# A gated DeltaNet layer: convolution taps in PSUM, triangular solve on blocks of 16, and an earlier place for the solve

## The chip, the cores and the metric

The kernel runs on one core of one Trainium2 chip. The metric is the device time of one execution in microseconds (us). Before the change three runs took 1976.09, 1970.93 and 1973.98 us, median 1973.98.

## The reference

A two-layer backbone on 640 tokens (128 of a context, 512 of a sample), width 1024. Layer 0 mixes with a state-space model and attention, layer 1 with a bidirectional gated DeltaNet; an MLP follows each. The change lies in the DeltaNet:

```python
qkv = jax.nn.silu(_dwconv(proj[..., :3 * D_MODEL], conv_w))      # 5 taps along the tokens
q, k, v = split(qkv); q, k = l2norm(q) * DK ** -0.5, l2norm(k)
a_mat = jnp.where(tri_strict, (kb @ k.T) * decay, 0.0)           # per chunk, kb = k * beta
t_mat = triangular_solve(eye + a_mat, eye)                       # (I + A)^-1
u_c, w_c = t_mat @ (v * beta), t_mat @ (kb * exp(gcum))
# per chunk, in order:
v_new = u_i - w_i @ s
o = (q_i * exp(g_i)) @ s + attn_i @ v_new
s = s * exp(g_last) + (k_i * exp(g_last - g_i)).T @ v_new
out = (rmsnorm(o) * silu(z)) @ w_out
```

There are 8 heads of 128 and two directions, forward and backward.

## The kernel before

All tokens are columns: an activation is a set of tiles of 128 features by 640 tokens. A projection (`gemm`, `mm_step`, L205 to L207) splits weights and activations in a high and a low fp32r part and makes three matmuls of 320 columns per pair of 128x128 weight block and half; a tile of 128 outputs takes 48 of them. `weight` (L193 to L196) loads a block, ScalarE rounds the high part (L194), POOL forms the low one (L196).

The layer's method `odd` lets 33 tiles of the in-projection run: tile 0 holds the gates, 1 to 24 are four pairs of heads with six tiles each (`gdn_project`: k, k, q, q, v, v, m = 0 to 5), 25 to 32 are the gate z (`zproj`). For each pair, in words of the code:

- `gdn_project.ev` takes a tile from its PSUM bank ("pg") to `cb`, runs the five taps of the convolution there (L1319 ScalarE, L1322 VectorE, on 642 columns), for some tiles one tap through ScalarE and POOL (L1325, L1326), then tanh (L1328) and the closing multiply, on POOL for m 2 and 3 (L1332, L1333), else on VectorE (L1335, L1336). Then come square sums (L1272), normalising (L1278, L1285, L1290) and transposes to token order (L1299).
- `gdn_group` makes, for each chunk of 128 tokens, four matrices (two heads, two directions): Gram products (L1395), decay (L1400, L1401) and transposes (L1407). The strictly triangular 32x32 diagonal blocks go to `ub`, 80 of them on 80 partitions.
- `gdn_blocks` inverts these blocks by 31 steps of one multiply (L1425) and one subtract (L1427) on VectorE and stores them (`dd`, L1431).
- `gdn_inverse` loads them (`gcm`, L1439), spreads them over block-diagonal tiles by a mask on POOL (L1453) and transposes on VectorE (L1454), and merges 32 to 64 to 128 by small matmuls (helper at L1458) with ScalarE copies between.
- `gdn_chain` runs the chunks: `prep` (L1562 to L1579; the decay of the queries is multiplied on POOL at L1567), and per link L1615, L1620 (VectorE), L1625, L1627 (ScalarE), L1631 and L1632, L1643, L1646 (VectorE). A link needs the state that the link before it leaves.

Behind the z tiles the `gated` products (L1680 to L1689) are projected by `wouto`, four head tiles first and the rest in `odd_out`. Fillers (`mod_half`, L269, L282) load and compute the modulation of the MLP, 14 of them near the end of the layer.

No order is written out by hand. A tile scheduler sets each engine's order from data dependence and from priorities: groups are raised by 1000, the solve of blocks by 3000, inverse and chain by 10000, z tiles lowered by 3000 below that. The rings of the pools then decide when a tile is free: PSUM has the tags "pg", "pa", "pb" and "pc" with two banks each, SBUF has one ring per name with its `bufs`.

```python
for j in range(31):
    n, m = 31 - j, j + 1
    t = tmp[:, :n * m].rearrange("p (a b) -> p a b", b=m)
    V.tensor_tensor(t, ub[:, j, j + 1:32]..., D[:, j, 0:m]..., op=ALU.mult)
    V.tensor_tensor(D[:, j + 1:32, 0:m], D[:, j + 1:32, 0:m], t, op=ALU.subtract)
```

Of the kernel before, what the change touches and what calls it, by code (L numbers as in the profile page):

```python
# [11 lines left out]
F32 = mybir.dt.float32  # L12
# [8 lines left out]
T = 640  # L21
HB = 320
# [126 lines left out]
class Build:  # L149
# [1098 lines left out]
    def gdn_project(self, pr, hn, P, first=None, mid=None):  # L1248
# [45 lines left out]
        def tok(ty):  # L1294
            for part in range(3):
# [7 lines left out]
                if part < 2:  # L1303
                    nc.scalar.activation(dst[part][:, 1:5], pv, AF.Copy)
                else:
                    for hh in range(2):
                        V.tensor_copy(dst[hh][:, 0], pv[:, hh])
        def ev(m, h, p):
# [9 lines left out]
            cv = self.tl([128, 642], "cv")  # L1318
            nc.scalar.activation(cv, cb[m][:, 0:642], AF.Identity, scale=cw[:, 0:1])  # L1319
            split = m > 3 and pr > 0  # L1320
            for t in range(1, 4 if split else 5):
                V.scalar_tensor_tensor(cv, cb[m][:, t:t + 642], cw[:, t:t + 1], cv, op0=M, op1=AD)  # L1322
            if split:
                cy = cb[m][:, 4:646]
                nc.scalar.activation(cy, cy, AF.Identity, scale=cw[:, 4:5])  # L1325
                nc.gpsimd.tensor_tensor(cv, cv, cy, op=AD)  # L1326
            th = cb[m][:, 0:642]
            nc.scalar.activation(th, cv, AF.Tanh)  # L1328

            if m in (2, 3):  # L1330
                nc.scalar.activation(th, th, AF.Identity, bias=1.0)
                nc.gpsimd.tensor_tensor(cv[:, 0:128], th[:, 0:128], cv[:, 0:128], op=M)  # L1332
                nc.gpsimd.tensor_tensor(cv[:, 128:T], th[:, 130:642], cv[:, 130:642], op=M)  # L1333
            else:
                V.scalar_tensor_tensor(cv[:, 0:128], th[:, 0:128], 1.0, cv[:, 0:128], op0=AD, op1=M)  # L1335
                V.scalar_tensor_tensor(cv[:, 128:T], th[:, 130:642], 1.0, cv[:, 130:642], op0=AD, op1=M)  # L1336
# [78 lines left out]
    def gdn_blocks(self, pr, ub, P):  # L1415
# [18 lines left out]
    def gdn_inverse(self, pr, ud, dd, P):  # L1434
# [3 lines left out]
        cm = P.tile([128, 20, 32], F32, name="gcm")  # L1438
        nc.sync.dma_start(out=cm, in_=self.ap(dd, 0, [[32, 128], [4096, 20], [1, 32]]))  # L1439
# [5 lines left out]
        mask = self.cst[:, 404:532].rearrange("p (b j) -> p b j", b=4).unsqueeze(1).to_broadcast([128, 2, 4, 32])  # L1445

        D = P.tile([128, 5, 4, 128], F32, name="gD")
        TT = P.tile([128, 5, 4, 128], F32, name="gTT", bufs=2)
        two = lambda t, c, d: t[:, c, 2 * d:2 * d + 2].rearrange("p u j -> p (u j)")
        for c in range(5):  # L1450
            for d, a, b in ((0, D, TT), (1, TT, D)):
                src = cm[:, 4 * c + 2 * d:4 * c + 2 * d + 2].unsqueeze(2).to_broadcast([128, 2, 4, 32])
                G.tensor_tensor(a[:, c, 2 * d:2 * d + 2].rearrange("p u (b j) -> p u b j", b=4), src, mask, op=ALU.mult)  # L1453
                V.transpose(two(b, c, d), two(a, c, d))  # L1454
        CH = [(c, hh) for c in range(5) for hh in range(2)]

        def mm(out, l, r, col):
            nc.tensor.matmul(out, l, r, start=True, stop=True, tile_position=(0, col))  # L1458

        def bank(n):  # L1460
            return self.ps("pb")[:, :320].rearrange("p (c h j) -> p c h j", c=5, h=2)


        p = bank(0)
        for c, hh in CH:
            for a in (0, 64):
                x, y = slice(a, a + 32), slice(a + 32, a + 64)
                mm(p[y, c, hh], uo[:, 0, c, hh, a:a + 32], D[:, c, hh, x], a + 32)
# [53 lines left out]
    def gdn_chain(self, pr, pd, TT, P, roles, bank):  # L1522
# [23 lines left out]
        def prep(t):  # L1546
# [9 lines left out]
            if t:  # L1556
# [9 lines left out]
                for u in range(4):  # L1566
                    nc.gpsimd.tensor_tensor(gq[:, u], gq[:, u], lds[u][2 + u % 2], op=M)  # L1567
# [432 lines left out]
```

## Time and profile before

| | us |
|---|---|
| median of three runs | 1973.98 |
| the profiled execution | 1975.42 |
| its span, first to last instruction | 1973.2 |
| TensorE busy in the span | 1798.4 |
| the DeltaNet layer, first tile to the next statistics | 882.3 to 1502.5 |
| in it: TensorE busy | 533.3 |
| in it: VectorE busy | 456.8 |
| in it: ScalarE and POOL busy | 288.4, 284.8 |

One execution was profiled. Engines are PE (TensorE), DVE (VectorE), ACT (ScalarE), POOL and SP; PE's weight loads (PEld) run beside its matmuls. Busy time of matmuls counts overlapping records, so a busy PE may still be short of work; the start of one record to the start of the next shows its pace. An fp32 matmul leaves two records. A wait for several semaphores is put down to the last one.

### The profile page before, as it was taken

Reading aid. Unit: us, or ns where it says so; the run is one execution under the profiler, and the core shown is the slowest. Engines: PE = TensorE matmul, PEld = TensorE weight load, DVE = VectorE, ACT = ScalarE, POOL = GpSimd, SP = SyncE. Lnnn points to the kernel's source line nnn. Section 1 sums busy time; section 2 is a strip of 40 time slices with the busy share of each in tenths; the row PEclk is TensorE's granted clock in tenths of the full one; section 3 lists DMA queues with packets and bytes.
Section 4 is the critical chain, followed back from the end, with each engine's and each line's share of the span. In section 5 each row is a group of like instructions: output and inputs, shape, how many; then the busy total and the mean of one; then the engine's idle time right before and its main releaser. Section 6 shows DMA issues by size and latency. Waiting matters only on the chain. (4 is left out here: it accounts for less than half of the span.)

```text
span 1973.2 us, 35750 instructions
## 1 busy us (share of the span) xinstructions
PE 1798.4 (91%) x13556; PEld 1696.1 (86%) x13556; DVE 1279.3 (65%) x2797; ACT 875.5 (44%) x1956; POOL 760.1 (39%) x609
## 2 busy tenths in 40 slices
PE   5789799989999999997878888798989899999998
PEld 3789677978999999997877888787878799999997
DVE  8998777269273644547589988674667927364553
ACT  4344466344243443535454455344324425344362
POOL 2522101541343343453455555522245334343451
PEclk9989899999999999998998999999999999999999
DMA  8446886533332222332576468758844122222221
GB/s 319 131 122 167 248 264 205 201 121 126 109 117 76 77 85 82 135 117 72 163 208 197 117 196 239 222 166 269 274 137 149 54 97 76 86 76 86 76 97 54
DMA packets 206983, 286.60 MB, mean 145 GB/s; under 512 B 54878, under 2 KB 138236, under 8 KB 206812
## 3 DMA queue, kind: packets, MB, share of 16 engines
q1 hardware_dynamic: 206812, 284.33, 45.4%
q8 instruction: 107, 1.75, 0.4%
q14 instruction: 64, 0.52, 0.1%
HBM read 228.87 MB, written 46.82 MB: 140 GB/s over the span
## 5 line engine op out<-in xcount | busy, mean ns | idle before, releaser
L196 POOL TENSOR_TENSOR wlo<-raw,whi 128x1024 fp32r<-128x1024 f32 (+1 forms) x153 | 359.3, 2351 | 509.1 <-ACT whi L194 462.3
L194 ACT ACTIVATE whi<-raw 128x1024 fp32r<-128x1024 f32 (+1 forms) x153 | 153.1, 1001 | 329.1 <-PE pg L206 146.8
L207 PE MATMUL pg<-hidh,wlo 128*128 128x320 f32 (+2 forms) x576 | 178.8, 311 | 0.6 <-POOL wlo L196 0.6
L205 PE MATMUL pg<-hidh,whi 128*128 128x320 f32 (+2 forms) x576 | 179.0, 311 | 0.0
L206 PE MATMUL pg<-hidl,whi 128*128 128x320 f32 (+2 forms) x576 | 178.9, 311 | 0.0
L423 DVE SCALAR_TENSOR_TENSOR x<-pg,mod,x 128x128 f32<-128x128 f32 (+2 forms) x132 | 53.7, 436 | 182.2 <-PE pg L207 182.2
L205 PE MATMUL pg<-h10h,whi 128*128 128x320 f32 x472 | 158.4, 336 | 14.7 <-DVE cb L1722 7.0
L207 PE MATMUL pg<-h10h,wlo 128*128 128x320 f32 x472 | 155.4, 329 | 1.7 <-POOL wlo L196 1.7
L206 PE MATMUL pg<-h10l,whi 128*128 128x320 f32 x472 | 155.7, 330 | 0.0
L205 PE MATMUL pa<-hidh,whi 128*128 128x320 f32 x448 | 138.0, 310 | 1.1 <-ACT whi L194 1.1
L207 PE MATMUL pa<-hidh,wlo 128*128 128x320 f32 x448 | 138.4, 309 | 0.0
L206 PE MATMUL pa<-hidl,whi 128*128 128x320 f32 x448 | 138.2, 309 | 0.0
L423 DVE SCALAR_TENSOR_TENSOR x<-pa,mod,x 128x128 f32<-128x128 f32 (+2 forms) x108 | 43.9, 435 | 133.1 <-PE pa L207 133.1
L508 POOL TENSOR_TENSOR wq<-S,wq 128x512 fp32r<-128x512 f32 x52 | 71.3, 1371 | 115.3 <-ACT wq L507 115.3
L205 PEld LDWEIGHTS pg<-h10h,whi 128*128 128x128 f32 x472 | 95.8, 203 | 18.3 <-DVE cb L1722 8.0
L207 PEld LDWEIGHTS pg<-hidh,wlo 128*128 128x128 f32 x576 | 108.2, 188 | 1.6 <-POOL wlo L196 1.1
L205 PEld LDWEIGHTS pg<-hidh,whi 128*128 128x128 f32 x576 | 108.3, 188 | 0.9 <-issue 0.8
L206 PEld LDWEIGHTS pg<-hidl,whi 128*128 128x128 f32 x576 | 108.2, 188 | 0.4 <-DVE hidl L569 0.3
L1322 DVE SCALAR_TENSOR_TENSOR cv<-cb,cw,cv 128x642 f32<-128x642 f32 x90 | 95.8, 1065 | 10.4 <-ACT cv L1319 9.2
L207 PEld LDWEIGHTS pg<-h10h,wlo 128*128 128x128 f32 x472 | 95.4, 202 | 2.1 <-POOL wlo L196 1.9
L206 PEld LDWEIGHTS pg<-h10l,whi 128*128 128x128 f32 x472 | 95.7, 203 | 0.6 <-issue 0.4
L205 PEld LDWEIGHTS pa<-hidh,whi 128*128 128x128 f32 x448 | 83.9, 188 | 2.7 <-ACT whi L194 1.8
(743 smaller groups left out, 5745.4 us busy)
## 6 DMA issues: line engine op xcount, KB each, us to landing
raw<-in_wff SPq DMA_DIRECT2D x104, 512.0 KB
mraw<-in_wmod SPq DMA_DIRECT2D x96, 512.0 KB
raw<-in_wino SPq DMA_DIRECT2D x33, 512.0 KB
rawx<-in_wff SPq DMA_DIRECT2D x24, 512.0 KB
raw<-in_wine SPq DMA_DIRECT2D x16, 512.0 KB
cka<-pd SPq DMA_DIRECT2D x28, 256.0 KB
ckb<-pd SPq DMA_DIRECT2D x28, 256.0 KB
s5g<-s5g SPq DMA_DIRECT2D x32, 164.0 KB
```

The lines of the kernel that those rows point to most:

```text
L194: nc.scalar.activation(hi[:, :kt], raw[:, :kt], AF.Copy)
L196: (nc.vector if self.lov and self.nw % self.lov else nc.gpsimd).tensor_tensor(lo[:, :kt], raw[:, :kt], hi[:, :kt], op=ALU.subtract)
L205: nc.tensor.matmul(p[:, :n], hi[:, k], xh[:, s], start=(k == 0), stop=False)
L206: nc.tensor.matmul(p[:, :n], hi[:, k], xl[:, s], start=False, stop=False)
L207: nc.tensor.matmul(p[:, :n], lo[:, k], xh[:, s], start=False, stop=(k == kt - 1))
L423: nc.vector.scalar_tensor_tensor(x[m][:, s], p[:, ls], g, x[m][:, s], op0=ALU.mult, op1=ALU.add)
L508: (V if j % 2 else nc.gpsimd).tensor_tensor(t[:, 4:8], src, t[:, 0:4], op=SU)
L1322: V.scalar_tensor_tensor(cv, cb[m][:, t:t + 642], cw[:, t:t + 1], cv, op0=M, op1=AD)
```

## The change

1. The convolution's taps run on two pieces, 128 columns in SBUF (`cv`) and 512 in a bank of PSUM ("pc"). All taps and closing multiplies are on VectorE; no tap goes through ScalarE and POOL.
2. `gdn_blocks` inverts the two 16x16 diagonal blocks of each 32x32 block, both in one instruction, in 15 steps. The result has a tile of its own, `ubd`; `ub` has one buffer in place of two.
3. `gdn_inverse` loads the blocks and their off-diagonal parts by 14 loads, merges 16 to 32 by matmuls of 32x32 and makes the steps to 64 and 128 from compact tiles; no mask and no products on POOL.
4. The decay of the queries is multiplied on VectorE, two instructions of 256 columns in place of four of 128 on POOL.
5. The solve of a pair is emitted with its last tile (m = 5), and its inverse and chain at tile m = 1 of the next pair, ahead of that pair's Gram blocks.
6. The z tiles use `zth` (one buffer with the tag `ubd`), the modulation fillers use the buffers of `ub` and `ubd`, and the gated products use other tiles.

```diff
+        def conv(x, cw):
+            cv = self.tl([128, 642], "cv")
+            cl = self.ps("pc")
+            parts = ((cv[:, 0:128], 0), (cl, 130))
+            for o, c0 in parts:
+                nc.scalar.activation(o, x[:, c0:c0 + o.shape[1]], AF.Identity, scale=cw[:, 0:1])
+            for t in range(1, 5):
+                for o, c0 in parts[::-1]:
+                    V.scalar_tensor_tensor(o, x[:, c0 + t:c0 + t + o.shape[1]], cw[:, t:t + 1], o, op0=M, op1=AD)
+            for o, c0 in parts[::-1]:
+                nc.scalar.activation(x[:, c0:c0 + o.shape[1]], o, AF.Tanh)
+            for (o, c0), c1 in zip(parts[::-1], (128, 0)):
+                V.scalar_tensor_tensor(cv[:, c1:c1 + o.shape[1]], x[:, c0:c0 + o.shape[1]], 1.0, o, op0=AD, op1=M)
+            return cv
...
-        D = ub
-        for j in range(31):
...
+        D = P.tile([80, 32, 32], F32, name="ubd", bufs=1)
+        nc.gpsimd.memset(D, 0.0)
+        for j in range(15):
+            n, m = 15 - j, j + 1
+            sh = [80, 2, n, m]
...
+            V.tensor_tensor(t, both(ub, j, 1, j + 1, n)..., both(D, j, 1, 0, m)..., op=ALU.mult)
+            V.tensor_tensor(both(D, j + 1, n, 0, m), both(D, j + 1, n, 0, m), t, op=ALU.subtract)
...
+        px = [bank() for d in range(2)]
+        for d in range(2):
+            for n in range(10):
+                for r in S:
+                    mm(px[d][r, n], Gc[r, d, n], Dc[r, d, n], r.start, r.start)
+            ACT.activation(Xc[:, d], px[d], AF.Copy)
+        px = [bank() for d in range(2)]
+        for d in range(2):
+            for n in range(10):
+                for r in S:
+                    mm(px[d][r, n], Tc[r, d, n], Xc[r, d, n], r.start, r.start)
+            V.tensor_tensor(Dc[:, d], Dc[:, d], px[d], op=ALU.subtract)
+            V.transpose(fl(Tc[:, d]), fl(Dc[:, d]))
...
-                for u in range(4):
-                    nc.gpsimd.tensor_tensor(gq[:, u], gq[:, u], lds[u][2 + u % 2], op=M)
+                for d in range(2):
+                    V.tensor_tensor(gq[:, 2 * d:2 * d + 2], gq[:, 2 * d:2 * d + 2], lds[2 * d][8], op=M)
...
-            th = self.tl([128, HB], "cb")
+            th = zth[0][:, HB * h:HB * h + HB]
...
+            zth.append(P.tile([128, T], F32, name="zth", tag="ubd", bufs=1))
...
-            ub = P.tile([80, 32, 32], F32, name="ub", bufs=2)
+            ub = P.tile([80, 32, 32], F32, name="ub", bufs=1)
...
+                if m == 1 and held:
+                    solve(*held)
...
+                if m == 5:
+                    got.append(next(steps[0]))
             pd = self.gdn_project(pr, hn, P, first if pr == 0 else None, mid)
-            if held:
-                solve(*held)
-            held = pr, pd, steps[0]
+            held = pr, pd, got[0]
...
+                self.mraw = "", 0, [(P, "ub", 1), (P, "ubd", 1)]
```

What the scheduler makes of it is seen in the order of the instructions. The first place is TensorE (PE) at pair 0's inverse; L205 to L207 are the in-projection, L1458 (before) and L1463 (now) the inverse's small matmuls. Before, it stands among the matmuls of tile 19:

```order
L207 MATMUL pg<-h10h_8955,wlo 128x320
L1458 MATMUL pb<-gD,guf 32x32
L205 MATMUL pg<-h10h_8957,whi 128x320
L206 MATMUL pg<-h10l_8958,whi 128x320
L207 MATMUL pg<-h10h_8957,wlo 128x320
...
L1285 MATMUL pc<-cst,ktok 128x128 x2
...
L1272 MATMUL pc<-cst,tsq 128x2 x2
L1458 MATMUL pb<-gD,guf 32x32 x24
L1272 MATMUL pc<-cst,tsq 128x2
L206 MATMUL pg<-h10l_8962,whi 128x320
```

Now it stands between tile 11 and tile 12, as a row:

```order
L207 MATMUL pg<-h10h_8965,wlo 128x320
L1463 MATMUL pb<-gDc,gGc 32x32 x80
L1463 MATMUL pb<-gXc,gTc 32x32 x80
L1463 MATMUL pb<-gDc,guf 32x32
L1285 MATMUL pc<-cst,ktok 128x128 x8
L1463 MATMUL pb<-gDc,guf 32x32 x39
L1285 MATMUL pc<-cst,ktok 128x128 x2
L1463 MATMUL pb<-gGc,gTc 32x32 x20
L1463 MATMUL pb<-gTc,gGc 32x32 x40
L1463 MATMUL pb<-gD_10893,guf 64x64 x20
L1272 MATMUL pc<-cst,tsq 128x2 x3
L205 MATMUL pg<-h10h_8951,whi 128x320
```

The inverse moved ahead by seven tiles, and no matmul of the in-projection is left between its steps.

The second place is TensorE at a link of pair 2's chain; `ozh` and `ozl` are the gated products that `wouto` projects, `mraw` the modulation's weights. Before:

```order
L1625 MATMUL pa<-cR,gTT 128x128 x4
L292 MATMUL pc<-cst,mrow 128x128 x2
L1631 MATMUL pa<-cgq,cS 128x128
...
L1632 MATMUL pa<-cbc,cR 128x128
L205 MATMUL pg<-ozh_15936,whi 128x320 x2
L206 MATMUL pg<-ozl_15937,whi 128x320
L207 MATMUL pg<-ozh_15936,wlo 128x320
...
L1643 MATMUL pa<-cR,ckd 128x128 x4
```

Now, behind tile 25 and ahead of tile 26:

```order
L1646 MATMUL pa<-cS,cka 128x128 x4
L1656 MATMUL pa<-cR,gTT 128x128 x4
L1601 MATMUL pa<-cka 128x128 x2
L1662 MATMUL pa<-cgq,cS 128x128
...
L1663 MATMUL pa<-cbc,cR 128x128
L1674 MATMUL pa<-cR,ckd 128x128 x4
L1646 MATMUL pa<-cS,cka 128x128 x4
...
L1689 MATMUL pa<-cst,osq 128x2 x10
L1700 MATMUL pa<-cst,osc 10x128
L282 MATMUL pc<-mraw,scond 32x256 x4
L205 MATMUL pg<-h10h_8951,whi 128x320
```

The chain stood among projection matmuls of `wouto` and now stands by itself in front of a z tile.

The third place is VectorE (DVE) at the first steps of pair 0's solve. Before:

```order
L1425 TENSOR_TENSOR sbt<-ub 80x31
L1427 TENSOR_TENSOR ub<-ub,sbt 80x31
L1425 TENSOR_TENSOR sbt<-ub 80x60
L1427 TENSOR_TENSOR ub<-ub,sbt 80x30x2
L1425 TENSOR_TENSOR sbt<-ub 80x87
L1427 TENSOR_TENSOR ub<-ub,sbt 80x29x3
```

Now:

```order
L1428 TENSOR_TENSOR sbt<-ub,ubd 80x30
L1322 SCALAR_TENSOR_TENSOR cv<-cb,cv 128x128
L1318 SCALAR_TENSOR_TENSOR pc<-cb,cw,pc 128x512
L1430 TENSOR_TENSOR ubd<-ubd,sbt 80x2x15
L1428 TENSOR_TENSOR sbt<-ub,ubd 80x56
L1430 TENSOR_TENSOR ubd<-ubd,sbt 80x2x14x2
L1428 TENSOR_TENSOR sbt<-ub,ubd 80x78
L1430 TENSOR_TENSOR ubd<-ubd,sbt 80x2x13x3
```

Each step handles two blocks of 16 at once and there are 15 steps in place of 31; taps of the next pair's convolution, L1318 with its PSUM operand `pc`, stand between them.

## Rows read from the trace of the kernel before

**Rows 1.** Windows of the DeltaNet layer: stretch, length, busy us by engine, clock, DMA share.

```profile
882.30:1019.00 136.70, 115.98 (x755) 111.92 (x752) 96.04 (x178) 76.03 (x164) 62.23 (x77) 0.91 0.48 143
1019.00:1093.90 74.90, 60.13 (x380) 58.85 (x379) 72.23 (x127) 35.09 (x74) 42.87 (x40) 0.89 0.59 173
1093.90:1195.40 101.50, 85.82 (x888) 80.69 (x887) 94.30 (x212) 53.06 (x119) 63.49 (x66) 0.93 0.62 176
1195.40:1238.30 42.90, 39.55 (x441) 36.85 (x441) 34.09 (x100) 25.05 (x61) 17.21 (x22) 0.96 0.80 232
1238.30:1361.00 122.70, 102.99 (x1127) 95.98 (x1125) 79.44 (x215) 52.41 (x121) 48.72 (x49) 0.93 0.67 193
1361.00:1502.50 141.50, 128.82 (x1010) 114.78 (x1004) 80.73 (x226) 46.79 (x106) 50.26 (x57) 0.98 0.67 224
882.30:1502.50 620.20, 533.30 (x4586) 499.07 (x4582) 456.82 (x1055) 288.42 (x644) 284.78 (x310) 0.93 0.62 186
```

**Rows 2.** Timeline of TensorE, dense matmuls: start, duration, line, records.

```profile
1120.00 0.31 PE L207 MATMUL pg<-h10h,wlo 128*128 128x320 f32 x1
...
1120.29 0.31 PE L206 MATMUL pg<-h10l,whi 128*128 128x320 f32 x1
...
1121.77 0.87 PE L1458 MATMUL pb<-gTT,gcm 128*32 128x32 f32 x76
...
1362.02 1.39 PE L1458 MATMUL pb<-gTT,gcm 128*64 128x64 f32 x40
```

**Rows 3.** Waits of TensorE in the layer: us in total, times, longest.

```profile
PE pb L1458 <- DVE gD L1454: 6.7, 8, 1.5
PE pc L1299 <- DVE cv L1336: 6.3, 1, 6.3
```

**Rows 4.** VectorE, lines of the solve: groups with busy us and mean ns, then shortest/median/longest ns.

```profile
L1427 DVE TENSOR_TENSOR ub<-ub,sbt 80x31 f32<-80x31 f32 (+15 forms) x124 | 72.6, 585 | 1.6
L1425 DVE TENSOR_TENSOR sbt<-ub 80x31 f32<-80x31 f32 (+15 forms) x124 | 64.7, 522 | 1.8
...
L1425 DVE TENSOR_TENSOR sbt<-ub x124: 171/385/2614, 1021.6 to 1324.5; 80x31 f32<-80x31 f32 x8, 80x60 f32<-80x60 f32 x8, 80x87 f32<-80x87 f32 x8, 80x112 f32<-80x112 f32 x8
```

**Rows 5.** VectorE, convolution taps (busy us, mean), and three lines by shortest/median/longest ns.

```profile
L1322 DVE SCALAR_TENSOR_TENSOR cv<-cb,cw,cv 128x642 f32<-128x642 f32 x90 | 95.8, 1065 | 10.4 <-ACT cv L1319 9.2 <-DMA pd<-khT 0.7
...
L1335 DVE SCALAR_TENSOR_TENSOR cv<-cb,cv x16: 277/280/427, 922.6 to 1256.6; 128x128 f32<-128x128 f32 x16
...
L1336 DVE SCALAR_TENSOR_TENSOR cv<-cb,cv x16: 677/681/685, 922.8 to 1256.8; 128x512 f32<-128x512 f32 x16
...
L1400 DVE TENSOR_TENSOR gau<-pb,gbg x20: 674/678/692, 972.2 to 1253.0; 128x512 f32<-128x512 f32 x20
```

**Rows 6.** POOL's masks and decay multiplies, VectorE's transposes: shortest/median/longest ns.

```profile
L1453 POOL TENSOR_TENSOR gD<-gcm,cst x20: 716/727/1598, 1105.6 to 1343.0; 128x256 f32<-128x256 f32 x20
...
L1567 POOL TENSOR_TENSOR cgq<-cgq,cka x64: 444/458/1288, 976.8 to 1435.0; 128x128 f32<-128x128 f32 x64
...
L1454 DVE STREAM_TRANSPOSE gTT<-gD x20: 395/429/446, 1108.9 to 1348.6; 128x256 f32<-128x256 f32 x20
```

**Rows 7.** Timeline of SP and POOL: the solve's store and the first user of its reload.

```profile
1327.43 0.42 SPq L1431 DMA_DIRECT2D dd<-ub  x1
...
1337.51 0.72 POOL L1453 TENSOR_TENSOR gD<-gcm,cst 128x256 f32<-128x256 f32 x1 [9.15 <-DMA gcm<-dd]
```

**Rows 8.** Timeline of TensorE: one link of pair 2's chain.

```profile
1379.37 0.94 PE L1615 MATMUL pa<-cS,cka 128*128 128x128 f32 x6
...
1387.29 1.05 PE L1643 MATMUL pa<-cR,ckd 128*128 128x128 f32 x8
1388.18 0.61 PE L1570 MATMUL pa<-cka 128*128 128x128 f32 x4
...
1389.56 0.71 PE L1615 MATMUL pa<-cS,cka 128*128 128x128 f32 x4
```

**Rows 9.** SP's loads of the modulation weights: shortest/median/longest ns, first and last start.

```profile
L269 SPq DMA_DIRECT2D mraw<-in_wmod x14: 332/345/1311, 1367.7 to 1435.4; - x14
```

More of the change, by code (lines that the diff above doesn't have):

```diff
@@ L1317, in ev @@
             cw = self.cw[:, 6 * pr + m]
[L1318 to L1336, printed above, removed]
+            cv = conv(cb[m], cw)
             out[m] = cv
@@ L1455, in gdn_inverse @@
[L1455 to L1465, printed above, removed]
+        D64 = P.tile([128, 10, 64], F32, name="gD64")
+        fl = lambda t: t.rearrange("p n j -> p (n j)")
+        V.transpose(fl(Tc[:, 0]), fl(Dc[:, 0]))
+        V.transpose(fl(Dc[:, 1]), fl(Tc[:, 1]))
@@ new lines, in mm, with bank @@
+        def mm(out, l, r, row, col):
+            nc.tensor.matmul(out, l, r, start=True, stop=True, tile_position=(row, col))
+        def bank():
+            return self.ps("pb")[:, :320].rearrange("p (n j) -> p n j", n=10)
+        S = [slice(32 * k, 32 * k + 32) for k in range(4)]
+        px = [bank() for d in range(2)]
[4 more added lines that the diff above has]
+            ACT.activation(Xc[:, d], px[d], AF.Copy)
@@ L1466, in gdn_inverse @@
+        for d in range(2):
+            for r in S:
+                ACT.activation(TT[r, :, u2(d), r], ch(Tc[r, d]), AF.Copy)
+            for k in range(2):
+                r = S[2 * d + k]
+                ACT.activation(D64[r, :, 32 * k:32 * k + 32], Dc[r, d], AF.Copy)
+        p = bank()
+        for n in range(10):
+            c, hh = divmod(n, 2)
             for a in (0, 64):
                 x, y = slice(a, a + 32), slice(a + 32, a + 64)
[L1468 removed]
@@ new lines, in gdn_inverse @@
+        parts = ((0, 8), (8, 10))
+        for n0, n1 in parts:
+            p = self.ps("pb").rearrange("p (n j) -> p n j", n=8)
+            for n in range(n0, n1):
+                c, hh = divmod(n, 2)
+                mm(p[y, n - n0], uo[x, 0, c, hh, 32:96], D64[x, n], 0, 64)
+                mm(p[x, n - n0], uo[y, 1, c, hh, 0:64], D64[y, n], 64, 0)
+            ACT.activation(Y[:, n0:n1], p[:, :n1 - n0], AF.Copy)
+        for n0, n1 in parts:
+            p = self.ps("pb").rearrange("p (n j) -> p n j", n=8)
+            for n in range(n0, n1):
+                c, hh = divmod(n, 2)
+                mm(p[x, n - n0], Y[y, n], TT[y, c, hh, y], 64, 0)
+                mm(p[y, n - n0], Y[x, n], TT[x, c, 2 + hh, x], 0, 64)
+            ACT.activation(TT[x, n0 // 2:n1 // 2, 0:2, y], ch(p[x, :n1 - n0]), AF.Copy, scale=-1.0)
+            ACT.activation(TT[y, n0 // 2:n1 // 2, 2:4, x], ch(p[y, :n1 - n0]), AF.Copy, scale=-1.0)
@@ L1773, in odd @@
             nc.sync.dma_start(out=x[k], in_=xd[k])
-        zt = P.tile([128, 4, T], F32, name="gD")
+        zt = [P.tile([128, T], F32, name=n) for n in ("gTc", "gGc", "gXc", "gD64")]
         ot = P.tile([128, 3, T], F32, name="guf")
```

104 lines of the change are left out of this document (46 added, 58 removed).

## The prediction

> **What bounds the kernel now.** I read the page first: TensorE is by far the busiest engine, so time is what TensorE does plus what it waits. The change touches one stage, the gated delta rule (882 to 1502 us). Its windows [rows 1] are cut where TensorE begins tile 12, 18, 24 and 26 of the in-projection, ends tile 32, and begins the next norm's statistics; I counted 48 matmuls of L205 to L207 per tile to find these times. The reader is to see that VectorE is busy 72 of 75 us in the second window and 94 of 101 in the third, and only 57% to 79% elsewhere. So VectorE holds TensorE between tile 12 and 24, and something else does before and after.
>
> "Busy" overstates TensorE, since matmuls overlap. So I price its work by how soon the next one starts [rows 2]: two 320-wide matmuls from 1120.00 to 1120.29 give 0.146 us each; 76 records of the 32-wide inverse matmul take 0.87 us, 0.011 each, and a matmul is two records: I take 0.024; 64-wide 1.39/40, so 0.07 per matmul; 128-wide fp32 ones 0.89 us for 8 records, 0.222 per matmul [rows 8]. For the 2-wide sums and the modulations I take 0.2 and 0.17; they hardly differ between the kernels. With the counts from the program's order, the windows hold 109, 55, 79, 34, 89 and 131 us of work, 497 of 620. The rest, 28 + 20 + 23 + 9 + 34 + 10 = 123 us, is waiting and half clock: the granted clock averages 0.93 over the stage and 0.89 in the second window [rows 1]. The waits have no single cause [rows 3]: the largest of a long list are 6.7 us for the transposes of the inverse and 6.3 for the last multiply of a convolution.
>
> **The change part by part.**
>
> The solve. 124 multiplies and 124 subtracts cost VectorE 64.7 + 72.6 = 137.3 us in four pairs, 34 per pair. Single ones take from 171 ns to 2614 ns [rows 4], so other work stretches them. 30 instructions per pair stay, each on 30 to 128 elements; with the small ones at 171 ns and the median 385 ns, I take 0.25 us: 7.5 us per pair. VectorE loses 107 us (bounds: 88 at 0.4 us each, 117 at 0.17).
>
> The convolution. 90 taps of 642 columns cost 95.8 us, 16 closing multiplies in two parts, 0.68 and 0.28, 15.4 more [rows 5]. Now 24 tiles have five instructions of 512 columns at 0.68 and five of 128 at 0.28: 115 us, so +4 on VectorE. POOL and ScalarE lose the split tap and POOL the multiplies for two tiles of a pair. What is moved into PSUM is priced by two rows [rows 5]: a 512-wide instruction with an input in PSUM takes 678 ns, one on SBUF alone 681. [...] The cover is VectorE's new slack; without it the 4 us stand on the path. The new accumulators take the two "pc" banks in program order, and the key transposes and the square sums queue behind them: between 0 and 12 us (twice the 6.3 of [rows 3]); I take 0, since VectorE gets to them sooner, and 12 goes into the range.
>
> Masks and the decay multiply. POOL loses 40 masks at 0.73 and 64 multiplies at 0.46 [rows 6], 61 us, and gains memsets. VectorE loses 40 transposes at 0.43 (17 us), gains 16 of 320 columns at about 0.5 and 8 subtracts at 0.43 (11 us), and gets the multiplies as 32 of 256 columns at about 0.42 (between 0.28 and 0.68), 13 us. VectorE in all: 457 - 107 + 4 - 17 + 11 + 13 = 361 us of 620, nowhere the bound on average. ScalarE gains 12 copies of about 0.43 per pair, 20 us on 288: hidden.
>
> TensorE's added work: 160 matmuls of 32x32 per pair, 640 x 0.024 = 15 us; its bounds are 14 (0.011 per record) and 45 (the 64-wide price). The order's counts give 509 us in all, +13.
>
> Order on TensorE. Pair 0's inverse now stands in front of tile 12 (before: after tile 19), pair 1's at 18 (23), pair 2's at 24 (28), pair 3's at 26. Tile 12 cannot start until the inverse's rounds, each through ScalarE or VectorE and back, are over. The solve's result must go to memory and back first: store issued at 1327.4, first user at 1337.5 [rows 7], 10 us, and now in 14 loads on SP in place of 3. In the order the solve is five tiles ahead of its inverse (five tiles are over 35 us), so I take that part as covered. Pair 2's chain, formerly among the output projection's matmuls, stands alone behind tile 25: no matmul of a z tile between. One link takes 10.2 us at its best, 1379.37 to 1389.56 [rows 8], of which 24 fp32 matmuls are 5.3.
>
> By windows, work after (from the order): 119, 81, 88, 58, 75, 88 = 509. Rests that I expect:
> - before tile 12: 30 (28, less the 6 of the convolution's wait, plus 8 for pair 0's inverse without cover);
> - to 18: 8 (20, where VectorE was the bound; only half clock is left);
> - to 24: 13 (23, the same relief, less pair 1's inverse);
> - to 26 with chain 2 behind it: 27 (9, plus five links of about 10 us less 5 of work in each, 25, less what pair 2's relief gives back);
> - the z tiles: 8 (34; no convolution, no chain 2);
> - the tail: 5 (10, with chain 2 and nearly all of chain 3 gone from it).
> Sum 91, so 509 + 91 = 600 against 620: 20 us less. The profiled execution took 1975.4, so 1955.4; it stands 1.4 over the median of the runs, so **1954 us**. This case's own range is 1938 to 1966.
>
> The modulation loads are 14, from 1367.7 to 1435.4, 5.2 us apart [rows 9]. They again begin when the last solve frees its buffers; with one from each of two buffers I take the same pace, 73 us, inside the 93 us of the tail.
>
> **The rivals.**
>
> *More is freed than I count* (0.25). VectorE's queue stands behind many small waits; if it stops holding anything, the rest falls to the half clock, at most 0.07 x 620 = 43 us and, as TensorE stands for a part of it, some 35, plus chain 2's 25: about 60, so 509 + 60 = 569, -51: 1923, between 1905 and 1938. For it: the second window. Against: windows one, five and six, where VectorE wasn't the bound.
>
> *The inverses stand uncovered and it turns slower* (0.20). Before, gemm matmuls filled the rounds of an inverse; now TensorE waits in each. Six rounds through another engine at some 3 to 4 us are 20 to 25 us per pair for 6 of work. If the four cost 17 us each in place of the 8 to 10 that I have in the sums, the rest is 121 and the total 630, +10: 1984, up to 1995 with the banks' 12. It decides from about 15 us of standing per inverse. For it: the order, and 6.7 us of waits already in the inverse [rows 3]. Against: the gemm's own lead and VectorE's slack.
>
> *The end doesn't move* (0.13). If the modulation loads start later than the last z tile or come one at a time at twice 5.2 us, they end 73 to 146 us after 1390 and the statistics wait for them: 1968 to 1980, no change. For it: they share the solve's and the z tiles' buffer. Against: in the tail of now the DMA engines are busy 0.67 of the time [rows 1], so there is room for that pace.
>
> That the change doesn't do what it says has no case of its own: the solve's 30 instructions are in the order.
>
> **How the numbers follow.** Forecast 0.42, the others 0.25, 0.20 and 0.13. A change under 0.3% (6 us) can't be told from none. Faster by more: 0.41 of the forecast, 0.25, 0.03 of the third rival = 0.69; the same: 0.01 + 0.08 + 0.02 = 0.11; slower: 0.20. The range goes from 1912, in the first rival, to 1988, past the second's 1984: about 0.1 is left out at either end.
>
> **What would show it.** Right: VectorE at about 360 us in the stage with 120 solve instructions at 0.2 to 0.3 us; 512-wide taps at 0.68 us; tile 18 near 1120, tile 26 near 1260, a gap-ridden stretch of some 50 us behind tile 25; the statistics near 1482. Wrong: TensorE waiting over 15 us at an inverse, taps at 0.75 us, TensorE waiting for "pc" users in front of a Gram block, or modulation loads that end after the last z tile plus 90 us.

## The result: 2037 us, slower by 3.1%

The changed kernel took 2037.05 us (median), the kernel before 1974.78 in the same comparison: ratio 1.0314, interval 1.0293 to 1.0335, 62 us. The forecast was 20 us less, and the time lies outside its range. One of the four runs took 4025 us; the ratio leaves it out. The profiled execution took 2036.8 us with a span of 2035.0, 61.8 over that of before. The layers behind the DeltaNet take as long as before (471.7 against 470.9 us from the statistics to the end), so all of it is lost in this layer.

The windows of the changed kernel, cut at the same points as [rows 1] (tile 12, 18, 24 and 26, end of the z tiles, statistics), then the whole layer, then two stretches in it; columns as there:

```profile
881.50:1051.30 169.80, 133.80 (x1332) 126.18 (x1328) 124.04 (x278) 89.00 (x209) 62.31 (x76) 0.84 0.48 138
1051.30:1148.80 97.50, 84.11 (x779) 81.35 (x779) 68.41 (x196) 50.13 (x132) 31.18 (x37) 0.94 0.69 195
1148.80:1263.90 115.10, 95.90 (x1057) 90.32 (x1057) 76.20 (x215) 59.77 (x154) 33.25 (x37) 0.94 0.65 185
1263.90:1384.30 120.40, 78.57 (x1008) 71.39 (x1008) 55.33 (x182) 43.63 (x108) 17.18 (x17) 0.76 0.52 146
1384.30:1472.40 88.10, 82.06 (x1092) 79.33 (x1093) 32.23 (x64) 42.45 (x96) 13.18 (x6) 0.93 0.54 161
1472.40:1563.30 90.90, 83.06 (x599) 71.84 (x598) 45.72 (x125) 23.24 (x44) 40.79 (x30) 0.94 0.65 220
881.50:1563.30 681.80, 557.51 (x5859) 520.40 (x5856) 401.92 (x1056) 308.21 (x735) 197.88 (x203) 0.88 0.58 169
1019.40:1051.30 31.90, 23.92 (x643) 21.83 (x641) 19.20 (x49) 18.46 (x39) 7.27 (x9) 0.69 0.41 108
1286.40:1384.30 97.90, 58.64 (x597) 52.19 (x596) 41.43 (x138) 30.96 (x79) 15.92 (x12) 0.76 0.56 157
```

Two windows carry the loss: before tile 12 (169.8 us, 136.7 before, forecast 149) and tile 24 to 26 (120.4, 42.9 before, forecast 85). The two between them are 36 us longer than before, about the 35 us of work that the new order moved into them, where the forecast had them 14 us longer. The z tiles and the tail win 85 us back, as forecast (88 and 91 us, forecast 83 and 93). VectorE is busy 402 us where it was 457 and 361 was forecast: 55 of the 96 us of relief came, and they bought nothing in sum.

From here on I split the layer as the prediction did, but record by record: a full-speed price for each matmul record ([rows 2, 8]; for the 2-wide and the modulation estimates of 0.115 and 0.085 us, where overlapping records start a mean of 0.108 and 0.083 us before the next in the trace before), what a record takes beyond it at half clock (0.50 granted, as from 1032.3 to 1033.5 us in the changed kernel), and the rest as stall. Before: 462 us of work, 30 of half clock, 128 of stall. Changed: 476, 42 and 163. So 14 us more work, 12 more half clock, 35 more stall. The level of the work moves by some 8 us with the prices that one takes; these differences don't.

TensorE in front of tile 12, from its timeline; the last column is the wait before the row and what ended it:

```profile
1027.99 0.31 PE L207 MATMUL pg<-h10h,wlo 128*128 128x320 f32 x1
1030.25 1.08 PE L1463 MATMUL pb<-gDc,gGc 32*32 32x32 f32 x80 [1.95 <-DMA gDc<-dd]
...
1036.01 0.92 PE L1463 MATMUL pb<-gXc,gTc 32*32 32x32 f32 x53 [1.06 <-issue]
...
1042.22 0.55 PE L1463 MATMUL pb<-gDc,guf 32*32 32x32 f32 x24 [2.34 <-issue]
...
1049.36 0.70 PE L1463 MATMUL pb<-gD,guf 64*64 64x64 f32 x8 [1.29 <-ACT gTT L1517]
...
1051.28 0.61 PE L205 MATMUL pg<-h10h,whi 128*128 128x320 f32 x1
```

From 1028 to 1051.28 no in-projection matmul starts, and the granted clock averages 0.69 from 1019.4 to 1051.3: an in-projection record took 0.31 us at 1027.99, with 1.00 granted, and takes 0.61 at 1051.28, with 0.50. In pair 2's chain (a link took 10.2 us before, [rows 8]) and behind it TensorE stands still:

```profile
1310.93 0.61 PE L1601 MATMUL pa<-cka 128*128 128x128 f32 x4
1318.35 0.98 PE L1646 MATMUL pa<-cS,cka 128*128 128x128 f32 x3 [6.81 <-DMA cS<-in_sdn]
...
1369.91 0.38 PE L1700 MATMUL pa<-cst,osc 128*10 128x128 f32 x1 [3.14 <-DVE osc L1697]
1382.48 1.08 PE L282 MATMUL pc<-mraw,scond 128*32 128x256 f32 x8 [12.19 <-DMA mraw<-in_wmod]
1384.29 0.63 PE L205 MATMUL pg<-h10h,whi 128*128 128x320 f32 x1 [0.73 <-DVE zth L1753]
```

The 12.19 us stand in front of a filler: its weights go into the buffer of `ub`, which pair 3's solve leaves at 1378. The z tile behind it could not have started its evacuation sooner either, since `zth` is the solve's result tile:

```profile
1378.26 0.36 SPq L269 DMA_DIRECT2D mraw<-in_wmod  x1
1378.73 0.38 SPq L1432 DMA_DIRECT2D dd<-ubd  x1
...
1383.27 0.77 ACT L1752 ACTIVATE zth<-pg 128x320 f32<-128x320 f32 x2 [12.62 <-DMA dd<-ubd]
```

And the instructions of VectorE, with shortest, median and longest ns:

```profile
L1318 DVE SCALAR_TENSOR_TENSOR cv<-cb,cw,cv x96: 309/351/2445, 906.2 to 1273.2; 128x128 f32<-128x128 f32 x96
L1318 DVE SCALAR_TENSOR_TENSOR pc<-cb,cw,pc x96: 716/751/757, 931.3 to 1300.9; 128x512 f32<-128x512 f32 x96
...
L1322 DVE SCALAR_TENSOR_TENSOR cv<-cb,cv x24: 275/286/2076, 910.4 to 1274.8; 128x128 f32<-128x128 f32 x24
L1322 DVE SCALAR_TENSOR_TENSOR cv<-cb,pc x24: 649/680/689, 936.4 to 1302.3; 128x512 f32<-128x512 f32 x24
...
L1428 DVE TENSOR_TENSOR sbt<-ub,ubd x60: 178/256/2357, 1009.1 to 1378.1; 80x30 f32<-80x30 f32 x8, 80x56 f32<-80x56 f32 x8, 80x78 f32<-80x78 f32 x8, 80x96 f32<-80x96 f32 x8
```

The solve's instructions answer to [rows 4]: 0.256 us (0.25 forecast). The taps answer to [rows 5]: 0.751 and 0.351 (0.68 and 0.28 forecast). All these are medians; single ones took up to 2.4 us.

### The profile page after: what moved, and what is told of

Its sections match the earlier page's. It is cut to its first block, busy times and chain, and to the rows that moved or that the text cites. A ratio compares the mean times of both kernels' runs of the same rounds, so it can differ in the third digit from the quotient of the medians.

```text
span 2035.0 us, 38372 instructions
## 1 busy us (share of the span) xinstructions
PE 1824.2 (90%) x14836; PEld 1718.7 (84%) x14836; DVE 1223.2 (60%) x2799; ACT 896.0 (44%) x2046; POOL 673.5 (33%) x503
## 5 line engine op out<-in xcount | busy, mean ns | idle before, releaser
L207 PE MATMUL pg<-hidh,wlo 128*128 128x320 f32 (+2 forms) x576 | 178.8, 311 | 0.6 <-POOL wlo L196 0.6
L205 PE MATMUL pg<-hidh,whi 128*128 128x320 f32 (+2 forms) x576 | 179.1, 311 | 0.0
L205 PE MATMUL pg<-h10h,whi 128*128 128x320 f32 x472 | 156.2, 331 | 1.1 <-DVE zth L1753 0.7
L207 PE MATMUL pg<-h10h,wlo 128*128 128x320 f32 x472 | 154.7, 328 | 0.0
L205 PE MATMUL pa<-hidh,whi 128*128 128x320 f32 x448 | 138.0, 310 | 1.1 <-ACT whi L194 1.1
L207 PE MATMUL pa<-hidh,wlo 128*128 128x320 f32 x448 | 138.4, 309 | 0.0
L207 PEld LDWEIGHTS pg<-hidh,wlo 128*128 128x128 f32 x576 | 108.2, 188 | 1.6 <-POOL wlo L196 1.1
L205 PEld LDWEIGHTS pg<-hidh,whi 128*128 128x128 f32 x576 | 108.3, 188 | 0.9 <-issue 0.8
L205 PEld LDWEIGHTS pg<-h10h,whi 128*128 128x128 f32 x472 | 95.1, 202 | 3.1 <-DVE zth L1753 1.6
L207 PEld LDWEIGHTS pg<-h10h,wlo 128*128 128x128 f32 x472 | 94.8, 201 | 0.1
L205 PEld LDWEIGHTS pa<-hidh,whi 128*128 128x128 f32 x448 | 83.9, 188 | 2.6 <-ACT whi L194 1.8
L207 PEld LDWEIGHTS pa<-hidh,wlo 128*128 128x128 f32 x448 | 84.0, 188 | 0.4 <-issue 0.4
```

The costliest lines, as they stand in the source:

```text
L205: nc.tensor.matmul(p[:, :n], hi[:, k], xh[:, s], start=(k == 0), stop=False)
L207: nc.tensor.matmul(p[:, :n], lo[:, k], xh[:, s], start=False, stop=(k == kt - 1))
```

## The experiments

All ratios are against the kernel before, run beside. The first theories were that z tiles tied to the solve's tile leave chain 2 alone (N), that the inverses in a row are the loss (I), and that the convolution is (C).

**Z tiles untied.**

```diff
-            th = zth[0][:, HB * h:HB * h + HB]
+            th = self.tl([128, HB], "cb")
```

> The changed kernel with one part undone: the z tiles evacuate into the ring of cb again, as before the change, and no longer into the tile that the solve uses. In the order the z tiles then stand among pair 2's chain links, and pair 3's inverse and chain move behind the last z tile. Theory N (no cover: z tiles tied to the last solve leave pair 2's chain alone on TensorE, 98 us from 1286 to 1384 with at most 59 busy): the stretch behind tile 25 loses 40 us or more and the time falls from 2037 to 1985-2005, unless pair 3's chain costs the same at the end. Theory I (the inverses in a row, 32 us in front of tile 12 alone, are the loss): nothing they do is touched, 2025-2037. Theory C (the convolution in PSUM holds the end): 2030-2037.

2037.2 us, ratio 1.0328 (1.0283 to 1.0373): no gain. The hole moved. Two windows, the z tiles behind tile 26 and the tail:

```profile
1302.60:1380.20 77.60, 75.48 (x585) 73.88 (x584) 35.84 (x89) 35.87 (x84) 24.57 (x14) 1.00 0.63 183
1380.20:1562.80 182.60, 125.50 (x1392) 108.54 (x1391) 80.55 (x233) 53.47 (x115) 39.63 (x30) 0.79 0.58 187
```

The z tiles now run beside chain 2 at full clock, and pair 3's solve, inverse and chain come after them, alone, at 0.79. TensorE still stands in front of the filler that waits for the solve:

```profile
1420.89 1.08 PE L282 MATMUL pc<-mraw,scond 128*32 128x256 f32 x8 [28.73 <-DMA mraw<-in_wmod]
```

N's time is missed, and the exception it made (pair 3's chain costs the same at the end) is what happened: cover was moved, not made.

**Inverse and chain late again.**

```diff
-                if m == 1 and held:
-                    solve(*held)
...
+            if held:
+                solve(*held)
             held = pr, pd, got[0]
```

> The changed kernel with one part undone: the inverse and the chain of a pair are emitted behind the next pair's projection again, not at its second tile; z tiles stay tied to the solve's tile. In the order the inverse of pair 0 is spread over tiles 12.4 to 13.9 and pair 2's from 25.4 on, and chain 2 has z tiles about it. Theory I (inverses in a row without cover): the 32 us stand in front of tile 12 goes to under 10, likewise at 18 and 24, and the time falls to 1995-2015. Theory N: chain 2 finds z tiles beside it, so the 98 us stretch goes too; 1985-2005. Theory C: 2025-2037.

2012.9 us, 1.0213 (1.0175 to 1.0250), 20 to 24 us less, a time inside I's range. But tile 12 still begins at 1047.8 with no inverse in front of it. So the inverse isn't what holds it, against I.

**Convolution in SBUF again.** The diff of `ev` reversed.

> The changed kernel with one part undone: the convolution's taps run in SBUF on 642 columns again, with the split tap and the two closing multiplies on POOL. Theory C (taps in PSUM, measured 751 ns each on 512 columns against the 680 that was forecast, and banks of the normalising steps taken): the time falls by 15 us or more, to 2000-2020. Theories N and I: VectorE is busy 401 of 680 us in the stage and not the bound, so 2030-2045.

2049.5 us, 1.0389 (1.0347 to 1.0432): slower still, above all three ranges, though tile 12 now begins at 1017.4. Tile 26 begins 194.6 us after tile 24.

**Convolution in PSUM alone, on the kernel before.**

> The kernel before with one part of the change alone: the convolution's taps in PSUM and SBUF as in the changed kernel. VectorE, already busy 72 of 75 us between tile 12 and 18, gets 24 x (4 x 0.75 + 0.68 + 4 x 0.35 + 0.29) = 129 us where it had 111. Theory C: slower than before by 10 to 25 us, 1985-2000. Theories N and I: within 8 us of before, 1968-1983.

1972.3 us, 1.0003 (0.9983 to 1.0022). C is wrong in the sum, but tile 12 begins at 1054.8 here too, 36 us late, and later windows win it back. The timeline shows why it is late:

```profile
1030.67 0.31 PE L207 MATMUL pg<-h10h,wlo 128*128 128x320 f32 x1
1037.53 2.46 PE L1285 MATMUL pc<-cst,ktok 128*128 128x128 f32 x10 [6.55 <-DVE ktok L1278]
```

and so do its waits up to there (in all, times, longest):

```profile
PE pb L1393 <- DVE gau L1398: 15.1, 4, 6.7
PE pc L1272 <- ACT tsq L1268: 7.0, 5, 2.8
PE pc L1285 <- DVE ktok L1278: 6.5, 1, 6.5
```

TensorE has run out of in-projection: it is left with normalising and Gram blocks. ScalarE, which empties the in-projection's banks, shows what stood in front. Its two starts of a convolution (L1314) come 12.5 us apart, and between them it copies the key transposes out of "pc" (L1287):

```profile
1027.60 0.41 ACT L1314 ACTIVATE cv<-cb,cw 128x128 f32<-128x128 f32 x1 [2.95 <-PE pc L1299]
...
1039.51 0.60 ACT L1287 ACTIVATE khT<-pc 128x512 f32<-128x512 f32 x1 [0.26 <-PE pc L1285]
1040.14 1.30 ACT L1314 ACTIVATE pc<-cb,cw 128x512 f32<-128x512 f32 x2
1049.53 1.28 ACT L1377 ACTIVATE gbg<-gbg,ngc 128x128 f32<-128x128 f32 x4 [8.09 <-POOL gbg L1374]
...
1053.37 0.26 ACT L1329 ACTIVATE cb<-pg 128x128 f32<-128x128 f32 x1
```

The next evacuation (L1329) comes at 1053.4, after 8 us more for POOL's decay. That gave a theory on the banks (P), tried below.

**Both undone: z tiles untied, inverse late.** The first two diffs.

> The changed kernel with two parts undone at once: z tiles back in the ring of cb, and inverse and chain emitted behind the next pair's projection. New theory O (order): emitted at the next pair's second tile, inverse and chain have a higher priority than that pair's Gram blocks, so pair 3's Gram blocks come at 1303 us where they stood at 1217 before; its solve and all that waits for it come as late, and whatever then stands uncovered (z tiles tied to the solve's tile, or pair 3's chain at the end) is only a question of place. O says that each undoing alone moves the hole and both together close it: 1965-1990. Rival K (the sum of parts): the late emission gave 24 us and the z ring nothing, so 2005-2018. Rival M (more small matmuls of 32x32 and 14 loads are the loss): 2000 or more.

2007.9 us, 1.0188 (1.0162 to 1.0215). The parts add (K), and M's range holds it too; O, that both together close the hole, misses by 18 us.

**Blocks of 16 alone.** The changed kernel with convolution, decay multiply, z ring and late inverse of before. The solve is still emitted with its pair's last tile, and the fillers' and the gated products' tiles are the changed kernel's: no run here undoes these.

> The kernel before with the solve on blocks of 16 alone: 15 steps in place of 31 with the inverse that belongs to it, its tile and the modulation's buffers; convolution, decay multiply, z ring and the place of inverse and chain as before. In the order pair 3's Gram blocks stand at tile 23 to 24 (24.5 to 26 before) and its inverse at 26.4 (32.2). Theory O: the solve itself is a gain when it isn't put ahead of the Gram blocks; VectorE loses about 100 us; 1940-1968. Rival M (the 640 added matmuls and the extra loads cost more than the steps save): 1978-2000.

1995.1 us, 1.0129 (1.0105 to 1.0153): slower by 24, M's side. VectorE is busy 391 us in the layer and not 457, yet the stall is 131 us (128 before):

```profile
882.30:1519.00 636.70, 549.42 (x5841) 510.38 (x5837) 391.24 (x905) 310.84 (x699) 257.20 (x288) 0.93 0.60 180
```

**With the decay multiply on VectorE.**

```diff
-                for u in range(4):
-                    nc.gpsimd.tensor_tensor(gq[:, u], gq[:, u], lds[u][2 + u % 2], op=M)
+                for d in range(2):
+                    V.tensor_tensor(gq[:, 2 * d:2 * d + 2], gq[:, 2 * d:2 * d + 2], lds[2 * d][8], op=M)
```

> As the kernel with blocks of 16 alone, and the decay multiply on VectorE too (32 x 0.42 = 13 us there, 64 x 0.46 = 29 us less on POOL). Theory O: within 6 us of the one with blocks of 16 alone, since VectorE is no longer the bound; a rival, that VectorE's queue between links is what a chain waits for: 8 us or more slower than it.

1982.0 us, 1.0063 (1.0042 to 1.0083): 13 us better, where a tie or a loss was expected. The stall is some 118 us here.

**Early inverse alone, on the kernel before.** 31 steps, but the solve emitted at m = 5 and inverse and chain at m = 1.

> The kernel before with one part of the change alone: the solve emitted with its own last tile and the inverse and chain at the next pair's second tile, all else as before (31 steps). In the order pair 2's and pair 3's Gram blocks then fall behind the last z tile. Theory O: much slower, 2040 or more, pair 3's Gram blocks past 1330 us. Rival I (only the inverses in a row matter): here the inverses stand as spread as before, so 1975-2000.

2102.9 us in its only run. Pair 3's Gram blocks come at 1410 to 1421 us (1217 to 1239 before). Their first record before, here, and in the changed kernel:

```profile
1217.06 0.72 PE L1395 MATMUL pb<-khT 128*128 128x128 f32 x5
...
1410.45 0.71 PE L1395 MATMUL pb<-khT 128*128 128x128 f32 x4 [1.08 <-ACT gTT L1505]
...
1303.57 0.61 PE L1394 MATMUL pb<-khT 128*128 128x128 f32 x4
```

The place costs 132 us with the long solve and some 20 with the short one and the other parts; that the solve's length makes the difference is likely, not shown.

**Convolution in PSUM, other banks.**

```diff
-            cl = self.ps("pc")
+            cl = self.ps("pa")
```

> The kernel before with the convolution in PSUM, its accumulators in the banks tagged pa (the chains') and not pc (the normalising steps'). Theory P (bank): with pc, a tap can't start until the normalising steps of the pair have left a bank, the in-projection's evacuation stands behind the taps, and TensorE has only square sums, transposes and Gram blocks in a row: tile 12 begins at 1055 us where it began at 1019. With pa, tile 12 begins before 1030 and the stalls before it fall from 47 us to 30 or less. The chain's links then take their turn for the same banks, so the whole time is open: 1950-1985. Rival Q (what delays tile 12 is the longer taps on VectorE, 751 and 351 ns): tile 12 stays at 1045 or later.

Tile 12 begins at 1006.8, the stall before it is 15 us (47 with "pc", 24 before): P is right and Q wrong. The whole is 2037.3 us, 1.0333 (1.0313 to 1.0352), above the range given for it, since the next window pays, with one wait of 31.2 us for POOL's mask:

```profile
1006.80:1177.90 171.10, 105.73 (x897) 99.23 (x896) 123.82 (x333) 57.27 (x144) 50.47 (x70) 0.77 0.49 139
```

```profile
PE pb L1456 <- POOL gD L1451: 31.2, 1, 31.2
```

**Decay multiply alone.**

> The kernel before with the decay multiply on VectorE alone. On the kernel with blocks of 16 this step gave 13 us. Theory L (POOL's place in the link is what costs: its queue stood 45 us behind the copies of the last decay): here too a gain, 1955-1966. Rival V (VectorE full between tile 12 and 24, so it gains only where the solve is short): 1970-1985.

1968.4 us, 0.9977 (0.9965 to 0.9990): 4 us faster, between the two theories; POOL's busy time falls by 35 us, VectorE's rises by 18.

**Convolution in PSUM and decay multiply.**

> The kernel before with convolution in PSUM and decay multiply on VectorE, no other part. If the parts add up, as the decay multiply alone does; Theory L: 1955-1968; Rival V: 1972-1990.

1988.1 us, 1.0080 (1.0059 to 1.0100), in V's range. Parts don't add: 0 and -4 make +16.

**Convolution and place undone, z tiles still tied.**

> The changed kernel with two parts undone, the convolution and the place of inverse and chain; z tiles remain tied to the solve's tile. It differs from the kernel with blocks of 16 and the decay multiply on VectorE (1982) by that tie alone. Theory O: with the Gram blocks in time the tie costs little, 1982-1990. Rival (the tie is the main loss whatever the place): 2005 or more.

1984.6 us, 1.0058 (1.0037 to 1.0078), as without the tie (1.0063): with the Gram blocks in time the tie costs nothing that can be told.

**VectorE's load taken away.** The kernel before with 15 of 31 steps:

```diff
-        for j in range(31):
+        for j in range(15):
```

> The kernel before with the solve cut to its first 15 steps (it leaves out steps 16 to 31 of the triangular inverse); VectorE loses over 60 us of work, TensorE gets none. Theory W (VectorE's load holds TensorE between tile 12 and 24, as the prediction said): the stalls there fall and the time goes to 1940-1955. Theory S (stalls come from the order and from single late inputs, not from VectorE's load): 1962-1978.

1959.0 us, 0.9914 (0.9884 to 0.9944), between the two theories: 14 us by the medians, 17 by the ratio. The layer, then tile 12 to 18 and 18 to 24:

```profile
882.50:1484.90 602.40, 524.64 (x4559) 492.88 (x4556) 415.80 (x925) 284.62 (x643) 273.50 (x308) 0.93 0.63 190
1017.40:1105.20 87.80, 68.82 (x677) 65.03 (x676) 79.32 (x146) 42.12 (x91) 48.80 (x52) 0.90 0.65 179
1105.20:1214.30 109.10, 95.40 (x888) 91.11 (x888) 91.91 (x200) 57.51 (x140) 54.45 (x66) 0.92 0.70 199
```

VectorE is busy 416 us in the layer, 41 less (over 60 were expected). Its load held TensorE, but by 0.35 to 0.4 us per microsecond, and not where theory W had it: by the split above, stall and half clock between tile 12 and 24 are some 55 us (some 50 before), and what was won lies behind tile 26 (42 after 58).

**Blocks of 16 without the merge from 16 to 32.** The two rounds `px` removed from the kernel of 1982 us.

> The kernel with blocks of 16 and the decay multiply on VectorE (1982), without the merge from 16 to 32 (it leaves out the two rounds of 80 small matmuls per pair, with their two copies, two subtracts and two transposes). If the added TensorE work and the two rounds are what blocks of 16 cost: 1982 less 640 x 0.023 = 15 us of matmuls and some waiting, 1955-1968. Rival (the cost lies in the 14 loads and the tiles that they wait for): 1975-1985.

1956.6 us, 0.9911 (0.9876 to 0.9946). Against its parent, 1.52 points, 30 us, with the two intervals 22 to 38. The layers of the two, with the merge and without:

```profile
882.60:1505.50 622.90, 541.81 (x5841) 508.64 (x5837) 401.22 (x937) 311.83 (x699) 227.62 (x224) 0.92 0.62 184
```

```profile
882.10:1479.20 597.10, 522.11 (x4561) 489.94 (x4557) 403.76 (x921) 308.24 (x691) 231.29 (x224) 0.93 0.64 192
```

1280 records fewer, 25.8 us less: 14.5 of work, 3.7 of half clock, 7.7 of stall.

**Gram blocks first.** The early place stays, the Gram blocks are raised over it.

```diff
-                with tc.high_priority(offset=1000):
+                with tc.high_priority(offset=20000):
                     self.gdn_group(pr, c, pd, P, ub, ud, pd["ed"])
```

> The changed kernel with one number changed: the Gram blocks' priority is raised by 20000 and not by 1000, so they stand ahead of the inverse and the chain of the pair before, which keep their early place. In the order pair 3's Gram blocks then stand at tile 23.5 to 24.3 (26.0 in the changed kernel) and pair 2's chain spreads over tiles 23.9 to 26. Theory O (that the solve stands in front of the Gram blocks is the loss): pair 3's Gram blocks before 1265 us and 1985-2012. Theory N (z tiles tied to the solve's tile leave the chain alone whatever the Gram blocks do): 2025 or more.

2013.3 us, 1.0189 (1.0153 to 1.0225): 22 to 25 us better, a microsecond above O's range and far from N's. Pair 3's Gram blocks came at 1286 us, though, and not before 1265: 17 us earlier than in the changed kernel. The first of them:

```profile
1286.39 0.83 PE L1394 MATMUL pb<-khT 128*128 128x128 f32 x6
```

The window of tiles 24 and 25 shows what went:

```profile
1295.30:1350.60 55.30, 43.94 (x311) 39.53 (x309) 39.49 (x118) 21.55 (x56) 14.55 (x12) 0.97 0.91 258
```

55 us at clock 0.97 for 120 at 0.76. The windows around it pay a part back: tile 12 to 18 takes 123 us for 97.5, the z tiles 96 for 88.

**Gram blocks first, z tiles untied.**

> As the one with the Gram blocks first, and z tiles back in the ring of cb. Theory O: with the Gram blocks in time the tie costs little, within 8 us of the former. Theory N: 25 us or more under it.

1997.9 us, 1.0118 (1.0086 to 1.0149), 15 us better than with the tie: between O and N. Pair 3's Gram blocks come at 1281 us here, still late, and then the tie does cost.

**Gram blocks first on the kernel with the decay multiply.**

> The kernel before with the decay multiply on VectorE (1968) and the Gram blocks raised ahead of inverse and chain. In the order pair 1's Gram blocks come a tile later and pair 2's and 3's about one tile sooner. Theory O: the Gram blocks are in time here already, so little is left to gain, 1960-1972. A rival, that Gram blocks ahead of a chain's links delay the chain, which ends the layer: 1978 or more.

1962.4 us, **0.9957 (0.9941 to 0.9974)**: 9 us faster than before and the lowest of the complete versions here, though its interval overlaps that of the decay multiply alone. It takes two things, the decay multiply from the change and the Gram blocks' priority from the experiments.

## Why the prediction was wrong

By the prediction's own sum the layer was to take 600 us and took 681.8. Taking its work from each window, the rests miss by 21 us before tile 12 (51 for 30), 23 between tile 12 and 24 (44 for 21), 35 from tile 24 to 26 (62 for 27), 5 in the z tiles and -2 in the tail. So three terms failed, those of steps 1, 3 and 4 below, and step 2 adds to them.

One path of parts, each kernel's median less that of before beside it: blocks of 16, +24; decay multiply, to +11; tied z tiles, to +12; convolution in PSUM, to +42; early place, to +62. In another order the parts have other prices (early place on the kernel before: +132; convolution on the kernel before: 0, and on the one with the early place some -15), so the path is an account, not a set of constants.

1. *VectorE holds TensorE between tile 12 and 24, and relief cuts the rest there from 43 us to 21.* This step failed: 44 us of rest were left, although VectorE's busy share in these windows fell from 94% to 68%. The 96% of the second window was read as a bound. VectorE did end most of TensorE's waits before, 21 of 30 us in these windows and 52 of 87 in the layer, and the relief took 10 and 14 us of them. Waits that a load ends took their place: 12 us where there were none, and in the layer 48 after 7. In these windows they are (us in all, times, longest):

```profile
PE pb L1463 <- DMA gDc<-dd: 5.1, 1, 5.1
...
PE pa L1646 <- DMA cS<-in_sdn: 4.0, 2, 2.1
...
PE pa L1601 <- DMA cka<-pd: 2.8, 3, 1.3
```

The first is the solve's result on its way back from memory, which the prediction took as covered. Taking 41 us of load away alone gave 14 to 17 us, and none of it between tile 12 and 24; taking more away with blocks of 16 alone left the stall where it was.

2. *160 matmuls per pair, 15 us.* Right as work: 14 us in the split of the layer. But the merge cost 26 us in the trace and 22 to 38 by the ratios, since each of its two rounds goes through ScalarE or VectorE and TensorE stood (7.7 us) or ran at half clock (3.7) in between. The term was mis-sized by that half, and it alone is more than the 14 to 17 us that less load on VectorE gave.

3. *The "pc" banks, 0 to 12 us, taken as 0.* This term failed too, shown by the other banks: stall before tile 12 of 47 us with "pc", 15 with "pa". The evacuation of the in-projection stands behind a tap that waits for a bank which the pair's normalising steps hold, and TensorE waits for the evacuation (ScalarE's rows above; 8 us of that wait are POOL's). I had looked at who queues behind the taps and not at what queues behind the evacuation. What it costs in the end was 0 on the kernel before and 30 us on the one with blocks of 16 and the late inverse.

4. *Early place; chain 2 alone, 27 us of rest.* The place and the missing cover were read rightly from the order, the price wasn't, and it is the largest miss: the window 24 to 26 held 55 us of work and 65 of stall and half clock, not 27. Left out were the state's load (6.8 us), the wait for pair 3's solve (12.2, seen at a filler), and the clock at 0.76. Raising the Gram blocks returned 22 to 25 us, as much as undoing the place. So the early place hurts by what it is put in front of; that it is due to the Gram blocks' lateness alone isn't shown, since they came only 17 us sooner.

5. *Taps at 0.68 and 0.28.* Measured 0.751 and 0.351, so 24 x 4 x 0.14 = 13 us more on VectorE by the medians. By their summed durations the convolution's instructions took 146 us and not 115, and the solve's 40 and not 30, which accounts for the 41 us by which VectorE's 402 exceed the forecast 361. I had taken the price from closing multiplies with a constant; a tap reads its factor from a tile. PSUM isn't needed for it: the 128-wide taps, on SBUF alone, are 65 ns longer too (351 against 286), and the closing multiply with an input in PSUM takes 680 ns here, 681 on SBUF before [rows 5]. The kernel before had the price as well, in its own taps on 642 columns of SBUF:

```profile
L1322 DVE SCALAR_TENSOR_TENSOR cv<-cb,cw,cv x90: 758/878/3014, 909.6 to 1246.8; 128x642 f32<-128x642 f32 x90
```

Its closing multiplies, 681 ns for 512 columns and 280 for 128, put 642 columns at an estimated 817 ns; the taps' median is 61 more.

6. *The decay multiply, hidden at 13 us on VectorE.* It was a gain of 4 us on the kernel before and 13 with blocks of 16. Why isn't settled.

7. *Modulation loads, no change.* The tail took 91 us where 93 was forecast. No run undoes the fillers' buffers alone.

Four slips of a microsecond or less in the prediction change nothing: the rests before add up to 124 us and not 123, the added work is 12 and not 13, the lower bound of the solve's relief is 89 and not 88, and TensorE's largest single cause of waiting was 7.0 us, for VectorE's step of the z tiles, and not 6.7.

The rival that turned slower named inverses without cover and +10 us; its sign and a part of its mechanism are what happened. For pair 0's inverse TensorE was without in-projection for 23 us, some 14 of them beyond its work. But undoing the place left tile 12 late (1047.8), and undoing the convolution with the inverse still early brought it to 1017.4, so the banks and not the inverse set that time.

## What to carry to other kernels

A busy share near 1 beside a bottleneck wasn't a bound here (VectorE 72 of 75 us; 41 us less load gave 14 to 17 us): cut the load in an experiment before paying for its relief with work on the bottleneck, and ask what the bottleneck will wait for next. When a change moves an accumulator into a shared ring of banks, follow the ring backwards, from who else holds a bank to what the waiting instruction is itself in front of, up to the engine that matters (here 47 us of stall with "pc", 15 with "pa"). And when a long serial part is given priority, look at what it is put ahead of; here one priority number returned a third of the loss.

## What the runs showed of the hardware

- A tap on VectorE whose factor comes from a tile takes 351 ns on 128 columns and 751 on 512, the multiply with a constant 286 and 680: some 65 to 70 ns more at either width. No run separates the factor's place from the rest.
- The matmuls on 32 rows and 32 columns took as long as those on 128 rows and 32 columns: 80 records take 0.89 us in the kernel with blocks of 16, against 76 in 0.87 before [rows 2], where the granted clock was 1.00. In the changed kernel 115 such records take 1.21 us from 1390.31 on, where it was 1.00, and 80 take 1.29 us at 1032.37, where it was 0.50. The 80 in 0.89 us:

```profile
1063.76 0.89 PE L1465 MATMUL pb<-gDc,gGc 32*32 32x32 f32 x80 [0.80 <-ACT gXc L1477]
```

- Behind pair 0's inverse, at a granted clock of 0.50, the first in-projection matmul took 0.61 us in place of 0.31. Over the layer the granted clock fell from 0.93 to 0.88, 12 us of TensorE's time by the split above. It was low in stretches where TensorE stood, 0.69 with 23.9 of 31.9 us busy (1019.4 to 1051.3) and 0.76 with 78.6 of 120.4 (1263.9 to 1384.3), and 1.00 over the z tiles of the first experiment, with 75.5 of 77.6 busy.
